# Two more heads in the Strassen products of one projection of a hybrid decoder layer

## The chip, the cores and the metric

The kernel runs on one core of a Trainium2 chip. The metric is the device time of one execution in microseconds (us). The kernel before takes 928.13 us, the median of three runs (927.85 to 928.35).

## What is computed

One layer of a trunk on 1024 tokens with 1024 channels: a state-space branch (S5) and a gated recurrent branch (RG-LRU, ten heads of 128 channels) are computed from one normalised input, projected, gated and added. The change concerns the projection of the second branch, `z_l`. From the reference, cut:

```python
s5_x, s5_g, lru_x, lru_g, gate_s, gate_l = jnp.split(proj, IN_SPLITS, axis=-1)
...
glu_a, glu_b = jnp.split(jax.nn.gelu(y_s) @ w_glu[i], 2, axis=-1)
y_s = glu_a * jax.nn.sigmoid(glu_b) * jax.nn.silu(s5_g)
z_s = y_s @ w_bs[i]
...
y_l = rg_lru(c, lru_w_a[i], lru_b_a[i], lru_w_x[i], lru_b_x[i], lru_lambda[i])
z_l = (y_l * jax.nn.silu(lru_g)) @ w_bl[i]
merged = jax.nn.sigmoid(gate_s) * z_s + jax.nn.sigmoid(gate_l) * z_l
x = x + rms_norm(merged @ w_out[i], g_post[i])
x = x + (p[i] @ w_ple[i]) * jax.nn.sigmoid(x @ w_ple_gate[i])
```

All data is float32, and `w_bl` has 1280 rows (ten heads) and 1024 columns.

## The kernel before, in words

Tensors lie with channels on the 128 partitions and the 1024 tokens along the free axis; a tile of 512 tokens is half a row (`HALF`). Matmuls run on rounded float32. To keep the precision, every operand is kept as a high part and a low part, the low one being the operand less its high part, and a product of two blocks is three matmuls of 128 x 128 by 128 x 512: high by high (L317), then high by low and low by high (L319), all in `three`. For activations `split` (L312, L313) makes the parts: ACT copies the high one, DVE subtracts for the low one.

**Weights.** A planner writes all weight blocks of 128 x 128 into one list and cuts it into quads of up to four blocks, in the order in which the products use them (`QUADS`). The class `Weights` brings each quad through four steps. `fetch` loads raw blocks on the SP queue into one of four raw buffers (a chunk of two blocks has a small buffer of its own). `sum` makes sums of raw blocks on POOL where Strassen's scheme wants them (L194). `make` puts the high part into one of six ring slots on ACT (L222). `lows` makes the low part on DVE (L234); for three weights behind the loop the low part comes from an accumulating DMA of POOL instead (L226). `next` hands out the quad that is due, `ahead` lets the steps run on by up to five quads. The instructions of all engines are in the order in which this code is written; only semaphores hold an engine back.

**The product with w_bl.** Heads 0 to 7 are seen as a matrix of two by two blocks: heads 0 to 3 and heads 4 to 7 in one direction, the two token halves in the other. Strassen's scheme in Winograd's form needs seven products for a pair of output rows. Each is over four blocks: 12 matmuls. Two of them, with operands B11 and B21, make a first stage (`bX`) that goes into the bank of psum `xs[p_]` for the four pairs p_; their sum is one output tile, and the first of them is kept in `bu`. The gated linear unit of the other branch comes in between (the GLU stage, `ysf`, `et`). Then a loop of four passes p_ does the other five products, with operands T2, T1, T3, B22 and T4, into banks z (`bZ`), w (`bW`) and v (`bV`). Behind T2, z gets `bu` added on DVE (L1322), and ACT copies it into u (L1323), which T3 needs as a start. Heads 8 and 9 are outside: `btail` adds their products, two blocks with six matmuls each time, to each output tile. Before the loop (`late_ops`) and while it runs, the operands T3, B22 and T4 are split, one tick at a time.

In one pass, PE does T2 (12 matmuls), T1 (12), the tail into v (6), T3 (12), the tail into w (6), B22 (12), the tail into z (6), T4 (12). DVE finishes output rows with `brow` (L1184), a product with the gates `ga` and `gb` that are read from DRAM.

```python
bprod(z, "T2", True)
V.tensor_tensor(z, z, u, ALU.add)
S.activation(u, z, AF.Copy)
bprod(w_, "T1", True)
S.activation(gb[:, HT:], w_, AF.Copy)
V.tensor_tensor(w_, w_, u, ALU.add)
tick()
...
btail(v, wb[2:], 1, True)
bmul(z, "T3", 2)
```

Gates for the stage of B11 and B21 are loaded from `sgl_d` on SP inside that stage, into tiles g0 and g1 of the pool `h2`. That pool's memory follows what was freed by the pool `l1` of the recurrent part.

Of the kernel before, what the change touches and what calls it, by code (L numbers as in the profile page):

```python
# [9 lines left out]
F32 = mybir.dt.float32  # L10
# [26 lines left out]
def weight_plan():  # L37
# [41 lines left out]
    for ks in (lo, hi2, hi):  # L79
        if ks is hi2:  # L80
            plain([b for m in range(0, ND, 2) for b in col("w_bl", m, hi2)])
            continue
        for m in (0, 4):
            plain(col("w_bl", m, ks) + col("w_bl", m + 2, ks))
    for j in range(NS):
        plain(col("w_glu", 4 + j, range(NS)) + col("w_glu", j, range(NS)))
    for m in range(0, ND, 2):
        c0, c1 = (chunk(col("w_bl", m + i, range(8))) for i in range(2))
        for part in ("O2", "S1", "P", "S3", "S4", "A22"):
            if part == "P":  # L90
                plain(col("w_bl", m, hi2) + col("w_bl", m + 1, hi2))
            else:
                quads.append((part, c0, c1, 4))
# [26 lines left out]
FIRST = ("O2",)  # L120


def chunk_users():
    last, begun = {}, {}
    for i, q in enumerate(QUADS):
        for c in q[1:2] if q[0] == "plain" else q[1:3]:
            if q[0] in FIRST or q[0] == "plain" and q[2] == 0:
                begun[c] = i
            last[begun[c], c] = i
    return last  # L130


LAST = chunk_users()


class Weights:
# [20 lines left out]
    def load(self, c):  # L157
        if c[1] == 2:
            t = self.tmp.tile([P, 2 * P], F32, tag="rawg", name=f"wraw{self.loads}")
        else:  # L160
            t = self.rawp.tile([P, 8 * P], F32, tag="raw", name=f"wraw{self.loads}")
        self.loads += 1
        self.nc.sync.dma_start(t[:, :c[1] * P], self.src[:, c[0] * P:(c[0] + c[1]) * P])
        return t

    def fetch(self, upto):
        while self.fetched <= min(upto, len(QUADS) - 1):
            q = QUADS[self.fetched]
            need = 2 if q[0] in FIRST else 1 if q[0] == "plain" and q[2] == 0 else 0
            small = need == 1 and q[1][1] == 2  # L170
            live = self.live[small] = [i for i in self.live[small] if i >= len(self.done) - len(self.owed)]
            if need + len(live) > (1 if small else self.RAW):
                return
            for c in q[1:1 + need]:
                live.append(LAST[self.fetched, c])
                self.raws[c] = self.load(c)
            self.fetched += 1

    def sum(self, upto):
        G = self.nc.gpsimd  # L180
        while len(self.ready) <= min(upto, len(QUADS) - 1):
# [14 lines left out]
            if q[0] == "plain":  # L196
                _, c, o, n = q
                self.ready.append((self.raws[c][:, o * P:(o + n) * P], n))
                continue
# [53 lines left out]
def tile_hybrid_trunk(  # L253
# [20 lines left out]
    page_pool = {i: pages for i in range(14)}  # L274
# [771 lines left out]
    yl, yl_raw = {}, {}  # L1046
    yr = []

    def yrow(k):
        if k % 2 == 0:  # L1050
            yr.append(page(6 + k // 2, f"yr{k // 2}", F32).rearrange("p (k n) -> p k n", k=2))
        return yr[k // 2][:, k % 2]
# [8 lines left out]
    def bq(q, k):  # L1061
        return yr[(k + 4 * (q // 20)) // 2][:, k % 2, HALF[q % 10 - 1]]

    def bsplit(name, k, src):
        hi, lo = bops[name]
        split(hi[:, k, :], lo[:, k, :], src)

    def lru_head(m):
# [33 lines left out]
        def late():  # L1102
# [11 lines left out]
            t = yrow(m) if m < 8 else l1.tile([P, NT], F32, tag=f"yr{m}", name=f"yr{m}")  # L1114
            V.tensor_tensor(t, sq, g, ALU.mult)  # L1115
            yl_raw[m] = t
# [32 lines left out]
    for m in (8, 9):  # L1149
        yl[m] = page(m - 4, f"yl{m}").rearrange("p (s n) -> p s n", s=2)  # L1150
        split(yl[m][:, 0], yl[m][:, 1], yl_raw[m])
# [21 lines left out]
    def bprod(ps, name, start):  # L1173
        W.ahead()
# [4 lines left out]
    def btail(ps, wb, h, start):  # L1179
        for k, w_ in zip((8, 9), wb):  # L1180
            three(ps, w_, (yl[k][:, 0, HALF[h]], yl[k][:, 1, HALF[h]]), start and k == 8, k == 9, not start)
# [17 lines left out]
    for p_ in range(4):  # L1199
        bprod(xs[p_], "B11", True)  # L1200
        S.activation(bu[:, p_, :], xs[p_], AF.Copy)
# [5 lines left out]
    for q in range(2):  # L1207
        W.ahead()
        wb = W.next()
        for i in range(2):  # L1210
            btail(xs[2 * q + i], wb[2 * i:2 * i + 2], 0, False)
# [9 lines left out]

    def t_ops():
        for k in range(4):
# [4 lines left out]
            V.tensor_tensor(bq(21, k), bq(21, k), t, ALU.subtract)  # L1228
            yield
        for k in range(4):  # L1230
# [46 lines left out]
    def late_ops():  # L1277
        for name, i, j, q in (("T3", 12, 13, 12), ("B22", 14, 15, 22), ("T4", 0, 1, 21)):
            bop(name, i, j)
            for k in range(4):  # L1280
                bsplit(name, k, bq(q, k))
# [28 lines left out]
    for p_ in range(4):  # L1310
# [9 lines left out]
        z, w_, v = (bank(f"b{n}{p_}") for n in "ZWV")  # L1320
        bprod(z, "T2", True)
        V.tensor_tensor(z, z, u, ALU.add)  # L1322
        S.activation(u, z, AF.Copy)  # L1323
        bprod(w_, "T1", True)
# [3 lines left out]
        W.ahead()  # L1328
        wb = W.next()
        btail(v, wb[2:], 1, True)  # L1330
        bmul(z, "T3", 2)
        S.activation(u, z, AF.Copy)
        V.tensor_tensor(v, v, gb[:, HT:], ALU.add)
        V.tensor_tensor(v, v, u, ALU.add)
        brow(m + 1, 1, ga[:, HALF[1]], v)
        tick()
        btail(w_, wb[:2], 1, False)
        bmul(w_, "B22", 2)
        brow(m, 1, gb[:, :HT], w_)
        tick()  # L1340
        btail(z, wb[2:], 0, False)
        bmul(z, "T4")
        brow(m + 1, 0, ga[:, HALF[0]], z)
# [354 lines left out]
```

## Time and profile before

| | |
|---|---|
| runs, median (low to high) | 928.13 us (927.85 to 928.35) |
| profiled execution | 928.25 us |
| its span | 926.5 us |
| PE busy | 919.0 us, 99% |
| DVE busy | 624.6 us, 67% |
| ACT busy | 469.1 us, 51% |
| POOL busy | 150.6 us, 16% |
| granted TensorE clock | 0.999 |

How to read it: the span is from the first to the last instruction of the profiled execution, and that execution took 1.75 us more than its span. Busy time is what the instructions of an engine cover. PE is TensorE's matmuls, DVE is VectorE, ACT is ScalarE, POOL is GpSimd, SP issues most of the DMAs. Numbers of lines, such as L313, are those of the kernel before.

### The profile page before, as it was taken

The page shows a single profiled execution, that of the slowest core. Times are in us where ns is not written, and L with a number is a line of the kernel's source. Part 1 is how long each engine was busy: PE and PEld are TensorE (multiplying, and loading weights), DVE is VectorE, ACT ScalarE, POOL GpSimd, SP SyncE. Part 2 cuts the span into 40 slices and gives each one's busy share as a digit, 9 for nine tenths or more (in the row PEclk, how much of TensorE's full clock was granted, in tenths as well). Part 3 has the DMA queues.
Part 4 walks back from the last instruction along what each step waited for, and adds up shares of the span by engine and source line. Part 5 has one row for each costly group of instructions (what it writes and reads, how often), then busy time and mean ns, then how long its engine had stood idle before and what let it go on. Part 6 is the DMA issues. An engine that isn't in the chain of part 4 may idle for free.

```text
span 926.5 us, 11716 instructions
## 1 busy us (share of the span) xinstructions
PE 919.0 (99%) x4228; PEld 760.3 (82%) x4228; DVE 624.6 (67%) x977; ACT 469.1 (51%) x714; POOL 150.6 (16%) x159
## 2 busy tenths in 40 slices
PE   9999999999999999999999999999999999999997
PEld 7888888888888888888888888888888887887886
DVE  6885566666664347766666767687862798886863
ACT  6643233444443356666666668544534355558531
POOL 1218112212220000000000000022322126422100
PEclk9999999999999999999999999999999999999999
DMA  9745445564533201111111116811479975499951
GB/s 358 277 126 160 126 142 166 172 171 133 173 97 113 74 29 52 52 46 51 52 52 52 47 34 216 291 56 55 141 255 244 247 193 206 119 245 233 301 184 56
DMA packets 70442, 134.21 MB, mean 145 GB/s; under 512 B 18416, under 2 KB 32880, under 8 KB 70384
## 3 DMA queue, kind: packets, MB, share of 16 engines
q1 hardware_dynamic: 64768, 122.72, 41.7%
q0 software_dynamic: 5472, 10.49, 6.3%
q8 instruction: 33, 0.54, 0.2%
q10 hardware_dynamic: 144, 0.26, 0.1%
q14 instruction: 25, 0.20, 0.1%
HBM read 95.30 MB, written 27.53 MB: 133 GB/s over the span
## 4 chain that ended last, share of the span: by engine, by line
PE 89%; issue 6%; DMA 2%; DVE 1%; POOL 1%; ACT 0%; POOLq 0%; SPq 0%
PE ps_L L319 16%; PE ps_L L317 8%; PE ps_rx L319 8%; PE ps_rg L319 8%; PE ps_rg L317 4%; PE ps_rx L317 4%; PE ps_F L319 3%; PE ps_u L319 3%; PE bZ L319 3%; PE ps_pg L319 2%; PE bW L319 2%; PE pg L319 2%; PE bX L319 2%; PE ps_ple L319 2%; PE ps_ea L319 2%
## 5 line engine op out<-in xcount | busy, mean ns | idle before, releaser
L319 PE MATMUL ps_L<-hB,wq 128*128 128x512 f32 x640 | 197.4, 390 | 0.0
L319 PEld LDWEIGHTS ps_L<-hB,wq 128*128 128x128 f32 x640 | 120.3, 188 | 24.3
L317 PE MATMUL ps_L<-hB,wq 128*128 128x512 f32 x320 | 127.1, 397 | 0.0
L222 ACT ACTIVATE wq<-wraw 128x512 fp32r<-128x512 f32 (+1 forms) x188 | 112.5, 613 | 24.1 <-issue 9.2
L234 DVE TENSOR_TENSOR wq<-wraw,wq 128x512 fp32r<-128x512 f32 (+1 forms) x152 | 105.0, 706 | 3.1 <-ACT wq L222 3.1
L319 PE MATMUL ps_rg<-hB,wq 128*128 128x512 f32 x320 | 98.5, 389 | 0.0
L319 PE MATMUL ps_rx<-hB,wq 128*128 128x512 f32 x320 | 98.5, 389 | 0.0
L319 PE MATMUL ps_pg<-x1hl,wq 128*128 128x512 f32 x240 | 74.9, 392 | 0.3 <-DVE x1hl L1374 0.2
L317 PEld LDWEIGHTS ps_L<-hB,wq 128*128 128x128 f32 x320 | 60.2, 188 | 13.3 <-issue 1.7
L319 PEld LDWEIGHTS ps_rg<-hB,wq 128*128 128x128 f32 x320 | 60.1, 188 | 12.5
L319 PEld LDWEIGHTS ps_rx<-hB,wq 128*128 128x128 f32 x320 | 60.1, 188 | 12.4
L194 POOL TENSOR_TENSOR wS<-wraw 128x512 f32<-128x512 f32 x8 | 12.4, 1549 | 354.8 <-DMA wraw<-w_blocks 343.3
L1078 DVE SCALAR_TENSOR_TENSOR c<-ps_rx,cp_t,c 128x1023 f32<-128x1023 f32 (+2 forms) x30 | 38.5, 1282 | 46.2 <-ACT c L1076 45.5
L317 PE MATMUL ps_rx<-hB,wq 128*128 128x512 f32 x160 | 62.3, 389 | 0.0
L317 PE MATMUL ps_rg<-hB,wq 128*128 128x512 f32 x160 | 62.3, 389 | 0.0
L319 PEld LDWEIGHTS ps_pg<-x1hl,wq 128*128 128x128 f32 x240 | 44.8, 188 | 11.5 <-DVE x1hl L1374 1.7
L1015 ACT ACTIVATE sg<-ps_L 128x1024 f32<-128x1024 f32 x20 | 20.5, 1027 | 59.7 <-issue 52.5
L226 POOL DMA_DIRECT2D wq<-wraw x36 | 31.8, 883 | 100.1 <-ACT wq L225 65.6
L317 PE MATMUL ps_pg<-x1hl,wq 128*128 128x512 f32 x120 | 47.0, 391 | 0.0
L319 PE MATMUL ps_u<-hB,wq 128*128 128x512 f32 x128 | 39.8, 392 | 0.4 <-DVE hB L736 0.4
L319 PE MATMUL ps_F<-ys,wq 128*128 128x512 f32 x128 | 39.4, 389 | 0.0
L1086 ACT ACT_TABLE_LOAD x9 | 11.5, 1283 | 51.2 <-DVE yr L1115 51.2
(360 smaller groups left out, 1927.0 us busy)
## 6 DMA issues: line engine op xcount, KB each, us to landing
wraw<-w_blocks SPq DMA_DIRECT2D x95, 512.0 KB
wq<-wraw POOLq DMA_DIRECT2D x36, 256.0 KB, 6.0
xt<-x_t SPq DMA_DIRECT2D x8, 512.0 KB
ple_d<-ple_sb SPq DMA_DIRECT2D x8, 512.0 KB
wn<-sbt SPq DMA_DIRECT2D x8, 512.0 KB
sgl_d<-sg SPq DMA_DIRECT2D x8, 512.0 KB
wn<-pt_d SPq DMA_DIRECT2D x16, 256.0 KB
sgs_d<-sg SPq DMA_DIRECT2D x8, 512.0 KB
```

Source lines behind the costliest of these rows:

```text
L194: G.tensor_tensor(s[name], s[a], s[b], op)
L222: nc.scalar.activation(hi, src, AF.Copy)
L226: nc.gpsimd.dma_start(lo.bitcast(F32), src, accum_op=ALU.add)
L234: self.nc.vector.tensor_tensor(lo, src, hi.bitcast(F32), ALU.subtract)
L317: T.matmul(ps, wh, xh, start=start, stop=False, skip_group_check=more)
L319: T.matmul(ps, a, b, start=False, stop=stop and a is (wh if xl_last else wl), skip_group_check=more)
L1015: S.activation(t, ps, AF.Sigmoid)
L1078: V.scalar_tensor_tensor(c[:, d:], ps[:, :NT - d], w_[3 - d], c[:, d:], ALU.mult, ALU.add)
L1086: S.activation(sq, ps, AF.Sigmoid)
```

## The change

Heads 8 and 9 become a fifth block of each of Strassen's seven products instead of plain tails: head 8 beside heads 0 to 3, head 9 beside heads 4 to 7. Each product is over five blocks, 15 matmuls, the last three by `bextra`. The tails in the loop and bank v go. The other operand of each product, the sum of heads, gets a fifth block in `bx` (page 19 holds heads 8 and 9, `yx`; the extra block of T4 stays in a psum bank, `t4x`). For the weights there are two new kinds of quads per pass: XS, four blocks of the extra block's sums, made by four operations on 128 x 128 on DVE one behind the other, and X22, the block alone. They come from two new small raw buffers of five blocks. The scratch of dynamic DMAs is 4096 bytes instead of its default of 16384, which moves all pools in SBUF down. The pool h2 no longer lies on l1's memory, and the four loads of gates in the stage of B11 and B21 move on the SP queue from that stage to right behind the stores of `y_d`. Cut to the core:

```diff
     hi2 = range(8, NL)
     for ks in (lo, hi2, hi):
         if ks is hi2:
-            plain([b for m in range(0, ND, 2) for b in col("w_bl", m, hi2)])
+            plain([("w_bl", k, m) for k in hi2 for m in range(0, ND, 2)])
...
     for m in range(0, ND, 2):
         c0, c1 = (chunk(col("w_bl", m + i, range(8))) for i in range(2))
-        for part in ("O2", "S1", "P", "S3", "S4", "A22"):
-            if part == "P":
-                plain(col("w_bl", m, hi2) + col("w_bl", m + 1, hi2))
-            else:
-                quads.append((part, c0, c1, 4))
+        cx = chunk([("w_bl", k, d) for k, d in ((9, m), (8, m), (8, m + 1), (9, m + 1))])
+        quads.extend((("O2", c0, c1, 4), ("XS", cx, 0, 4)))
+        quads.extend((part, c0, c1, 4) for part in ("S1", "S3", "S4", "A22"))
+        quads.append(("X22", cx, 3, 1))
...
+SINGLE = ("plain", "XS", "X22")
+
+
+def begins(q):
+    return 2 if q[0] in FIRST else int(q[0] in SINGLE and q[2] == 0)
...
 def chunk_users():
     last, begun = {}, {}
     for i, q in enumerate(QUADS):
-        for c in q[1:2] if q[0] == "plain" else q[1:3]:
-            if q[0] in FIRST or q[0] == "plain" and q[2] == 0:
+        for c in q[1:2] if q[0] in SINGLE else q[1:3]:
+            if begins(q):
                 begun[c] = i
             last[begun[c], c] = i
     return last
 LAST = chunk_users()
+SMALL = {q[1] for q in QUADS if q[0] == "XS" or q[1][1] == 2}
...
     def load(self, c):
-        if c[1] == 2:
-            t = self.tmp.tile([P, 2 * P], F32, tag="rawg", name=f"wraw{self.loads}")
+        if c in SMALL:
+            t = self.tmp.tile([P, 5 * P], F32, tag="rawg", name=f"wraw{self.loads}", bufs=2)
         else:
             t = self.rawp.tile([P, 8 * P], F32, tag="raw", name=f"wraw{self.loads}")
         self.loads += 1
+        if c[1] == 4 and c in SMALL:
+            for o, n in ((0, 3), (3, 1)):
+                self.nc.sync.dma_start(t[:, (o + o // 3) * P:(o + o // 3 + n) * P],
+                                       self.src[:, (c[0] + o) * P:(c[0] + o + n) * P])
+            return t
         self.nc.sync.dma_start(t[:, :c[1] * P], self.src[:, c[0] * P:(c[0] + c[1]) * P])
         return t
     def fetch(self, upto):
         while self.fetched <= min(upto, len(QUADS) - 1):
             q = QUADS[self.fetched]
-            need = 2 if q[0] in FIRST else 1 if q[0] == "plain" and q[2] == 0 else 0
-            small = need == 1 and q[1][1] == 2
+            need = begins(q)
+            small = need == 1 and q[1] in SMALL
             live = self.live[small] = [i for i in self.live[small] if i >= len(self.done) - len(self.owed)]
-            if need + len(live) > (1 if small else self.RAW):
+            if need + len(live) > (2 if small else self.RAW):
                 return
             for c in q[1:1 + need]:
...
+            if q[0] in SINGLE:
+                r = self.raws[q[1]]
+                if q[0] == "X22":
+                    self.ready.append((r[:, 4 * P:], 1))
+                    continue
+                a12, a11, a21, s1, a22 = (r[:, j * P:(j + 1) * P] for j in range(5))
+                for d, a, b, op_ in ((s1, a21, a22, ALU.add), (a21, a11, a21, ALU.subtract),
+                                     (a11, s1, a11, ALU.subtract), (a12, a12, a11, ALU.subtract)):
+                    self.nc.vector.tensor_tensor(d, a, b, op_)
+                self.ready.append((r[:, :HT], 4))
                 continue
...
-        if k % 2 == 0:
+        if k == 8:
+            yr.append(page(19, "yx", F32).rearrange("p (k n) -> p k n", k=2))
+        elif k % 2 == 0:
...
     def bq(q, k):
+        if k == 4:
+            return yr[4][:, q // 20, HALF[q % 10 - 1]]
         return yr[(k + 4 * (q // 20)) // 2][:, k % 2, HALF[q % 10 - 1]]
+    bx = {}
+
     def bsplit(name, k, src):
-        hi, lo = bops[name]
-        split(hi[:, k, :], lo[:, k, :], src)
+        split(*bx[name], src) if k == 4 else split(*(t[:, k, :] for t in bops[name]), src)
+
+    def bx_at(name, t, i):
+        bx[name] = t[:, i, :], t[:, i + 1, :]
...
-    for m in (8, 9):
-        yl[m] = page(m - 4, f"yl{m}").rearrange("p (s n) -> p s n", s=2)
-        split(yl[m][:, 0], yl[m][:, 1], yl_raw[m])
+    bx4, bx5 = (quarter(page(i, f"bx{i}")) for i in (4, 5))
+    bx_at("B11", bx4, 0)
+    bx_at("B21", bx4, 2)
+    bsplit("B11", 4, bq(11, 4))
+    bsplit("B21", 4, bq(21, 4))
+    V.tensor_tensor(bq(11, 4), bq(12, 4), bq(11, 4), ALU.subtract)
+    V.tensor_tensor(bq(12, 4), bq(22, 4), bq(12, 4), ALU.subtract)
...
-    def bprod(ps, name, start):
-        W.ahead()
+    def bprod(ps, name, start, held=1):
+        W.ahead(held)
         hi, lo = bops[name]
         for k, wb in enumerate(W.next()):
             three(ps, wb, (hi[:, k, :], lo[:, k, :]), start and k == 0, k == 3, not start)
-    def btail(ps, wb, h, start):
-        for k, w_ in zip((8, 9), wb):
-            three(ps, w_, (yl[k][:, 0, HALF[h]], yl[k][:, 1, HALF[h]]), start and k == 8, k == 9, not start)
+    def bextra(ps, wb, name):
+        three(ps, wb, bx[name], False, True, True)
...
         bprod(xs[p_], "B11", True)
-        S.activation(bu[:, p_, :], xs[p_], AF.Copy)
...
-    for q in range(2):
+    for name in ("B11", "B21"):
         W.ahead()
-        wb = W.next()
-        for i in range(2):
-            btail(xs[2 * q + i], wb[2 * i:2 * i + 2], 0, False)
+        for p_, wb in enumerate(W.next()):
+            bextra(xs[p_], wb, name)
+            if name == "B11":
+                S.activation(bu[:, p_, :], xs[p_], AF.Copy)
         tick()
...
+    t4x = []
+
     def t_ops():
-        for k in range(4):
+        bx_at("T2", bx5, 0)
+        for k in range(5):
             t = btmp[:, k % 2, :]
             V.tensor_tensor(t, bq(22, k), bq(11, k), ALU.subtract)
             bsplit("T2", k, t)
             yield
-            V.tensor_tensor(bq(21, k), bq(21, k), t, ALU.subtract)
-            yield
-        for k in range(4):
+            if k == 4:
+                t4x.append(px.tile([P, HT], F32, tag="px", name="t4x"))
+            V.tensor_tensor(t4x[0] if k == 4 else bq(21, k), bq(21, k), t, ALU.subtract)
+            yield
+        bx_at("T1", bx5, 2)
+        for k in range(5):
             bsplit("T1", k, bq(11, k))
...
     def late_ops():
         for name, i, j, q in (("T3", 12, 13, 12), ("B22", 14, 15, 22), ("T4", 0, 1, 21)):
             bop(name, i, j)
-            for k in range(4):
-                bsplit(name, k, bq(q, k))
+            if name == "T4":
+                bx_at(name, quarter(page(19, "bx19")), 0)
+            else:
+                bx_at(name, bx4, 0 if name == "T3" else 2)
+            for k in range(5):
+                bsplit(name, k, t4x[0] if name == "T4" and k == 4 else bq(q, k))
...
-        z, w_, v = (bank(f"b{n}{p_}") for n in "ZWV")
+        z, w_ = (bank(f"b{n}{p_}") for n in "ZW")
         bprod(z, "T2", True)
+        W.ahead()
+        wx = W.next()
+        bextra(z, wx[1], "T2")
         V.tensor_tensor(z, z, u, ALU.add)
         S.activation(u, z, AF.Copy)
-        bprod(w_, "T1", True)
+        bprod(w_, "T1", True, 2)
+        bextra(w_, wx[3], "T1")
         S.activation(gb[:, HT:], w_, AF.Copy)
         V.tensor_tensor(w_, w_, u, ALU.add)
         tick()
-        W.ahead()
-        wb = W.next()
-        btail(v, wb[2:], 1, True)
         bmul(z, "T3", 2)
-        S.activation(u, z, AF.Copy)
-        V.tensor_tensor(v, v, gb[:, HT:], ALU.add)
-        V.tensor_tensor(v, v, u, ALU.add)
-        brow(m + 1, 1, ga[:, HALF[1]], v)
+        bextra(z, wx[2], "T3")
+        V.tensor_tensor(gb[:, HT:], gb[:, HT:], z, ALU.add)
+        brow(m + 1, 1, ga[:, HALF[1]], gb[:, HT:])
         tick()
-        btail(w_, wb[:2], 1, False)
         bmul(w_, "B22", 2)
+        bextra(w_, wx[0], "B22")
         brow(m, 1, gb[:, :HT], w_)
         tick()
-        btail(z, wb[2:], 0, False)
         bmul(z, "T4")
+        W.ahead()
+        bextra(z, W.next()[0], "T4")
         brow(m + 1, 0, ga[:, HALF[0]], z)
...
-    nc = bacc.Bacc("TRN2", target_bir_lowering=False, num_devices=1)
+    nc = bacc.Bacc("TRN2", target_bir_lowering=False, num_devices=1, dynamic_dma_scratch_size=4096)
```

The instructions that the prediction speaks of stand on DVE. The first place is from the last product of the GLU stage (`ysf`) to the addition of `bu` into w (`bW`). In it `bT` is the low part of T3's operand, `bx` that of an extra block, `wq` the low part of a quad. Before:

```order
L1272 TENSOR_TENSOR ysf_4668<-et,ps_ea_4932 128x4x128
L1272 TENSOR_TENSOR ysf_4668<-et,ps_ea_4933 128x4x128
L313 TENSOR_TENSOR bT_4968<-yr_2940,bT_4967 128x512 x2
L313 TENSOR_TENSOR bT_4968<-yr_3277,bT_4967 128x512 x2
L234 TENSOR_TENSOR wq_4934<-wraw_4682,wq_4934 128x512
L1322 TENSOR_TENSOR bZ_4981<-bZ_4981,bu 128x512
L234 TENSOR_TENSOR wq_4984<-wS_120_4796,wq_4984 128x512
L234 TENSOR_TENSOR wq_5001<-wraw_4682,wq_5001 128x512
L1326 TENSOR_TENSOR bW_4982<-bW_4982,bu 128x512
```

and now:

```order
L1307 TENSOR_TENSOR ysf_4669<-et,ps_ea_4950 128x4x128
L1307 TENSOR_TENSOR ysf_4669<-et,ps_ea_4951 128x4x128
L334 TENSOR_TENSOR bT_4984<-yr_2942,bT_4983 128x512 x2
L334 TENSOR_TENSOR bT_4984<-yr_3279,bT_4983 128x512 x2
L334 TENSOR_TENSOR bx_4442<-yx,bx_4442 128x512
L255 TENSOR_TENSOR wq_4952<-wraw_4683,wq_4952 128x512
L255 TENSOR_TENSOR wq_5001<-wS_120_4798,wq_5001 128x512
L1364 TENSOR_TENSOR bZ_4999<-bZ_4999,bu 128x512
L1369 TENSOR_TENSOR bW_5000<-bW_5000,bu 128x512
```

A split of the extra block of T3 stands ahead, and the two quads' low parts stand ahead of the addition into z (`bZ`, L1364) instead of one; the raw quad's low part that stood third is later now.

The second place is behind it, up to the splits of T4: `bB` is B22's operand, `bT` is T4's, `ga` and `gb` the gates, `wraw` the raw weights. Before:

```order
L313 TENSOR_TENSOR bB_5024<-yr_3614,bB_5023 128x512 x2
L313 TENSOR_TENSOR bB_5024<-yr_3947,bB_5023 128x512 x2
L1333 TENSOR_TENSOR bV_4983<-bV_4983,gb_4978 128x512
L1334 TENSOR_TENSOR bV_4983<-bV_4983,bu 128x512
L1184 TENSOR_TENSOR ga_4977<-ga_4977,bV_4983 128x512
L313 TENSOR_TENSOR bT_5061<-yr_3614,bT_5060 128x512 x2
L313 TENSOR_TENSOR bT_5061<-yr_3947,bT_5060 128x512 x2
```

and now:

```order
L334 TENSOR_TENSOR bB_5042<-yr_3616,bB_5041 128x512 x2
L334 TENSOR_TENSOR bB_5042<-yr_3949,bB_5041 128x512 x2
L334 TENSOR_TENSOR bx_4442<-yx,bx_4442 128x512
L255 TENSOR_TENSOR wq_5016<-wraw_4683,wq_5016 128x512
L255 TENSOR_TENSOR wq_5053<-wraw_4685,wq_5053 128x128
L218 TENSOR_TENSOR wraw_4842<-wraw_4842 128x128 x4
L1373 TENSOR_TENSOR gb_4996<-gb_4996,bZ_4999 128x512
L1213 TENSOR_TENSOR ga_4995<-ga_4995,gb_4996 128x512
L334 TENSOR_TENSOR bT_5088<-yr_3616,bT_5087 128x512 x2
L334 TENSOR_TENSOR bT_5088<-yr_3949,bT_5087 128x512 x2
L334 TENSOR_TENSOR bx_5089<-t4x,bx_5089 128x512
```

Ahead of the splits of T4 there are now the low parts of two quads, the four chained operations on 128 x 128 (L218), and the addition of z into gb (L1373), on which the product with ga depends; the two additions into bank v are gone.

## Rows read from the trace of the kernel before

**Rows 1.** The page, first part: engine, busy us (share of the span), instructions.
```profile
span 926.5 us, 11716 instructions
PE 919.0 (99%) x4228; PEld 760.3 (82%) x4228; DVE 624.6 (67%) x977; ACT 469.1 (51%) x714; POOL 150.6 (16%) x159
```
**Rows 2.** PE's waits, first and last of five: line, releaser, us, times, longest us.
```profile
PE warm L500 <- DVE halfpi L291: 1.1, 1, 1.1
...
PE ps_pg L319 <- DVE x1hl L1374: 0.2, 1, 0.2
```
**Rows 3.** PE's timeline: start us, us, line and operation; loop's first matmul, first behind it.
```profile
637.83 0.39 PE L317 MATMUL bZ<-bT,wq 128*128 128x512 f32 x1
...
708.55 0.39 PE L317 MATMUL ps_F<-ys,wq 128*128 128x512 f32 x1
```
**Rows 4.** Windows: GLU stage, first, third, fourth pass: us; PE, PEld, DVE, ACT, POOL busy (count); clock.
```profile
600.00:637.00 37.00, 37.00 (x165) 30.67 (x164) 26.28 (x30) 17.43 (x27) 7.52 (x5) 1.00 0.22 74
637.80:655.50 17.70, 17.70 (x79) 14.64 (x78) 16.97 (x25) 9.07 (x17) 3.97 (x3) 1.00 0.16 50
...
673.20:690.90 17.70, 17.70 (x80) 14.66 (x79) 12.95 (x17) 6.70 (x12) 5.98 (x4) 1.00 0.68 224
690.90:708.50 17.60, 17.60 (x79) 14.60 (x78) 6.56 (x10) 7.74 (x14) 4.46 (x5) 1.00 0.93 265
```
**Rows 5.** DVE's timeline in the first pass: start us, us, instruction, [idle before, releaser].
```profile
639.47 2.47 DVE L313 TENSOR_TENSOR bT<-yr,bT 128x512 fp32r<-128x512 f32 x4
...
642.48 0.68 DVE L1322 TENSOR_TENSOR bZ<-bZ,bu 128x512 f32<-128x512 f32 x1
...
644.34 1.38 DVE L234 TENSOR_TENSOR wq<-wraw,wq 128x512 fp32r<-128x512 f32 x1 [0.59 <-ACT wq L222]
645.64 0.69 DVE L1326 TENSOR_TENSOR bW<-bW,bu 128x512 f32<-128x512 f32 x1
646.25 2.99 DVE L313 TENSOR_TENSOR bB<-yr,bB 128x512 fp32r<-128x512 f32 x4
649.16 0.69 DVE L1333 TENSOR_TENSOR bV<-bV,gb 128x512 f32<-128x512 f32 x1
649.95 0.70 DVE L1334 TENSOR_TENSOR bV<-bV,bu 128x512 f32<-128x512 f32 x1
650.69 0.69 DVE L1184 TENSOR_TENSOR ga<-ga,bV 128x512 f32<-128x512 f32 x1
```
**Rows 6.** ACT's timeline in the first pass: the copy of z.
```profile
643.19 0.60 ACT L1323 ACTIVATE bu<-bZ 128x512 f32<-128x512 f32 x1 [6.10 <-DVE bZ L1322]
```
**Rows 7.** POOL's timeline in the first pass: the second and third sum.
```profile
643.88 1.29 POOL L194 TENSOR_TENSOR wS<-wS,wraw 128x512 f32<-128x512 f32 x1 [12.15 <-issue]
645.14 1.74 POOL L194 TENSOR_TENSOR wraw<-wraw,wraw 128x512 f32<-128x512 f32 x1
```
**Rows 8.** Small operations on DVE: groups by shape (busy, mean ns), and one line's instructions.
```profile
L1615 DVE TENSOR_TENSOR sbp<-sbp,x 128x128 f32<-128x128 f32 x2 | 0.6, 292 | 0.1
...
L402 DVE TENSOR_SCALAR sdp<-ident,rs_pre x8: 279/283/287, 27.9 to 29.2; 128x128 f32<-128x128 f32 x8
```
**Rows 9.** DVE's timeline in the second pass: two low parts.
```profile
654.90 1.47 DVE L234 TENSOR_TENSOR wq<-wS,wq 128x512 fp32r<-128x512 f32 x1
...
660.57 1.11 DVE L234 TENSOR_TENSOR wq<-wraw,wq 128x512 fp32r<-128x512 f32 x1 [0.59 <-ACT wq L222]
```
**Rows 10.** SP's timeline: the stores of y_d and the next issue.
```profile
297.25 2.57 SPq L988 DMA_DIRECT2D y_d<-ysb  x4
304.39 0.33 SPq L1019 DMA_DIRECT2D sil_d<-sg  x1
```
**Rows 11.** The page: POOL's queue (packets, MB, share), issue cost by line, issue to landing.
```profile
q0 software_dynamic: 5472, 10.49, 6.3%
...
L226 POOL DMA_DIRECT2D wq<-wraw x36 | 31.8, 883 | 100.1 <-ACT wq L225 65.6
...
wq<-wraw POOLq DMA_DIRECT2D x36, 256.0 KB, 6.0
```
**Rows 12.** POOL's timeline in the second pass: the first sum.
```profile
659.73 1.40 POOL L194 TENSOR_TENSOR wS<-wraw 128x512 f32<-128x512 f32 x1 [3.91 <-DMA wraw<-w_blocks]
```

More of the change, by code (lines that the diff above doesn't have):

```diff
@@ L198, in sum @@
                 self.ready.append((self.raws[c][:, o * P:(o + n) * P], n))
+                continue
[3 more added lines that the diff above has]
+                    self.ready.append((r[:, 4 * P:], 1))
+                    continue
+                a12, a11, a21, s1, a22 = (r[:, j * P:(j + 1) * P] for j in range(5))
[3 more added lines that the diff above has]
+                self.ready.append((r[:, :HT], 4))
                 continue
@@ L273, in tile_hybrid_trunk @@
     pages = ctx.enter_context(tc.tile_pool(name="pages", bufs=1))
-    page_pool = {i: pages for i in range(14)}
+    page_pool = {i: pages for i in (*range(14), 19)}
     def page(i, name, dt=F32R):
@@ L1045, in tile_hybrid_trunk @@
     l1 = lctx.enter_context(tc.tile_pool(name="l1", bufs=1))
-    yl, yl_raw = {}, {}
     yr = []
     def yrow(k):
-        if k % 2 == 0:
+        if k == 8:
+            yr.append(page(19, "yx", F32).rearrange("p (k n) -> p k n", k=2))
+        elif k % 2 == 0:
             yr.append(page(6 + k // 2, f"yr{k // 2}", F32).rearrange("p (k n) -> p k n", k=2))
@@ L1113, in late @@
             yield
-            t = yrow(m) if m < 8 else l1.tile([P, NT], F32, tag=f"yr{m}", name=f"yr{m}")
-            V.tensor_tensor(t, sq, g, ALU.mult)
-            yl_raw[m] = t
+            V.tensor_tensor(yrow(m), sq, g, ALU.mult)
             yield
```

## The prediction

> **What bounds the kernel now.** I read the page first. TensorE (PE) is busy 919.0 of the 926.5 us span [rows 1], so the question is only how many matmuls are issued and how often the next one is late. The list of PE's waits answers the second half: five waits in the whole span, the longest 1.1 us, 2.8 us together (the first and the last are shown) and none of them in the w_bl loop [rows 2]. There PE runs without a gap: the first matmul of the loop starts at 637.83, the first of the stage behind it at 708.55, and between them lie 4 x 78 = 312 matmuls [rows 3], so one costs (708.55 - 637.83) / 312 = 0.2267 us. This is the price of a matmul below; the 0.39 us of a row is a modelled, overlapping length.
>
> The windows by pass then show who could stop PE. In the first pass of the loop DVE is busy 16.97 of 17.70 us; in the third it is 12.95 and in the fourth 6.56 [rows 4]. So the first pass has hardly any room on DVE, and the later ones have 4.7 us or more. The rest rests on DVE's own timeline in that first pass.
>
> A measurement of this kernel can tell about 0.2% from no change, 1.86 us; I use that as the bound of "same".
>
> **Part 1: the matmuls.** In the stage of B11 and B21 the count is the same: four tails of two blocks become eight blocks, 24 matmuls either way. In the loop a pass had five products of four blocks (T2, T1, T3, B22, T4: 60 matmuls) and three tails of two blocks (18), together 78. Now it has five products of five blocks: 75. Three fewer in each of four passes: 12 x 0.2267 = **-2.72 us**. PE is full there, so all of it is on the path.
>
> **Part 2: the third product of the first pass (T3).** T3 stands behind 30 matmuls before and after (12 + 12 + 6; now 15 + 15), so it is due at 637.83 + 30 x 0.2267 = 644.63 [rows 3], as before. Its first matmul adds into z and has to wait for ACT's copy of z to u. Before, DVE left the GLU product at 639.47, made T3's four splits in 2.41 us (0.60 each), one low part, and started z's add at 642.48 [rows 5]; ACT began the copy at 643.19, 0.71 us after that start, and took 0.60 [rows 6]. It was ready at 643.79, so 0.84 us early. Now a fifth split and the low part of S4's quad stand ahead of z's add (first pair of pieces in the section on the change): 639.47 + 5 x 0.60 + 2 x 0.60 = 643.68, and the copy is ready at 643.68 + 0.71 + 0.60 = 644.99. With the 0.04 us that the semaphore takes T3 starts at 645.03: **+0.4 us**, between 0.3 and 0.5.
>
> **Part 3: the last product of the first pass (T4).** It stands 30 matmuls behind T3: due at 645.03 + 6.80 = 651.83. Its first matmul now waits for the new addition of z into gb (DVE reads z, PE overwrites it), its second for the low part of T4's first split. DVE's queue up to there, second pair of pieces:
> - w's add waits for ACT's copy of w to gb, which can't start before T1's last matmul has ended and the copy of z is over (644.93); 0.60 us on, it starts at 645.53 (before 645.64 [rows 5]).
> - B22's splits from 646.13. Before, four took 2.91 us (646.25 to 649.16) where 2.41 would do; the 0.50 us is the third POOL sum, which ran until 646.88 [rows 7]. For five I take 3.01 plus 0.26 (half, since the sum may start earlier or later): 649.4.
> - the low part of A22's quad 0.60, that of the single block X22 0.19, which is the distance at which independent operations of that size start (eight from 27.9 to 29.2 [rows 8]): 650.2.
> - the four operations on 128x128 that make the extra block's sums, each waiting for the one before. A tensor_tensor of that size lasts 0.292 us [rows 8]; a dependent successor starts 0.04 to 0.10 us after the end (649.95 + 0.70 to 650.69, 649.16 + 0.69 to 649.95 [rows 5]). At 0.33 each 1.3 us: 651.5.
> - the addition of z into gb, 0.69 us: 652.2. T4's first matmul starts 0.4 us late.
> - ga's product depends on that addition and starts at 651.5 + 0.79 = 652.3, T4's first split at 652.9, ready at 653.55. T4's second matmul, due at 652.06, starts at 653.6. From there DVE gives a split every 0.60 us and PE uses one every 0.68, so nothing more is lost.
>
> Together **+1.5 us**. If the POOL sum no longer meets the splits and the four small operations follow each other without a gap (0.19 each) it is 0.7; if the sum costs 0.75 and each small operation 0.39, 2.2. I take 1.5, since the gaps between dependent operations are measured.
>
> A rule bears on the stretch. The row says that the low part which started at 644.34 lasted 1.38 us instead of 0.67 [rows 5], while POOL ran its sum from 643.88 to 645.17 [rows 7]; operations with a PSUM operand, such as w's add (0.69), were not stretched. The Trainium skill (SBUF — State Buffer, section "SBUF: two separate sides") states that VectorE and GpSimd share a port pair as an exclusive lock, held for the whole instruction, and that a VectorE operation with two SBUF inputs has to wait for a GpSimd operation that reads SBUF. The trace agrees: 643.88 + 1.29 to the end of 644.34 + 1.38 leaves 0.55, one undisturbed operation. By that rule, part 4 would be 0.4 us instead of 0, and the sum 0.4 us later.
>
> **Part 4: the passes behind it.** The backlog of the first pass enters the second: T4's splits end at 655.8, then two products, three low parts, the product with z, a split of ys and two low parts stand ahead of z's add, which comes at about 661.5 and lets T3 go at about 662.8 to 664.0 (POOL sums took 0.8 and 0.4 us from two such low parts [rows 9]). T3 of the second pass is due at 653.6 + 44 x 0.2267 = 663.5. So 0, at most 0.5. The third and fourth pass have 4.7 and 11 us of idle DVE [rows 4]: 0.
>
> **What costs nothing, and what hides it.** Behind the loop nothing is changed but the queue position of the next weights; no PE wait stood there. In the GLU stage DVE gets four more 512-column operations (2.4 us) and ACT two: DVE was idle 37.00 - 26.28 = 10.7 us there [rows 4]. Without that cover they would delay T2's first matmul by up to 2.4. ACT loses a copy of z in each pass and gets three splits in the first. On SP the extra block's load is two transfers instead of one, and four loads of gates move from the B11 stage to right behind the y stores; SP issued nothing there from 299.8 to 304.4 [rows 10].
>
> **Sum.** -2.72 + 0.4 + 1.5 + 0 = -0.8 us. The profiled execution took 928.25 us, 0.12 above the median of the runs (928.13). It becomes 927.4, on the median **927.3 us**. With the bounds (0.3 to 0.5, 0.7 to 2.2, 0 to 0.5) the forecast's own range is 926.4 to 928.6.
>
> **Rivals.**
> A: no stall. If DVE's work reaches T3 and T4 in time, because it leaves the GLU stage earlier than at 639.47 (its last operations there may come sooner) and POOL's sums fall elsewhere, the whole 2.72 us stays: 925.4 on the median. For it: PE waited nowhere in the loop, and my chain adds up seven estimates. Against it: DVE had 0.73 us of room in the first pass [rows 4], and three splits (1.8), a new addition in place of two (-0.7), and the four sums (1.3) are added to it. Chance 0.22.
>
> B: the quarter of scratch limits POOL's transfers. 36 low parts for the stages behind the loop are made by POOL's accumulating DMAs, 256 KB and 6.0 us each from issue to landing, 0.88 us to issue [rows 11]. A quad of w_bs feeds 24 matmuls, 5.44 us of PE. If only one such transfer could be in flight, a quad would come every 6.9 us, 1.45 us late: 8 quads of w_bs cost 11.6 us (939), all 36 cost 52 (979). From two in flight it costs nothing. No row tells how much of the scratch a transfer takes; the only one near it is the count of packets, 5472 / 36 = 152 a transfer over 16 engines [rows 11], about 10 each. Chance 0.05. The Trainium skill (DMA: Bandwidth & Descriptors, "Terms") has descriptors of 16 bytes, written to rings in SBUF; by it 4,096 bytes would hold 256 of them, an estimate, and B would not come about; no run here shows it.
>
> C: slower, by one wait that repeats. The four sums of the extra block are in DVE's queue, where POOL's stood in its own. If their raw block lands late, everything behind them on DVE waits: gb's addition, T4's splits, and so PE. In the second pass POOL's first sum waited 3.91 us for raw weights [rows 12], so loads there can be just in time. A stall like part 3's largest in each pass, 4 x 1.9 = 7.6, gives 928.25 - 2.72 + 7.6 = 933.1. It decides from 0.68 us a pass (slower than before at all) and 1.15 (by more than the bound). Against it: the extra blocks have two buffers of their own, and so are asked for more than a pass ahead. Chance 0.07.
>
> **Chances.** Forecast 0.62, A 0.22, B 0.05, C 0.07, and 0.04 for what I do not see, counted as no change. The range takes in the forecast and A: 925.2 to 928.7. Faster by over 0.2% (below 926.27): A and 0.03 of the forecast, 0.25. Slower by over 0.2% (above 929.99): B and C, 0.12. Same: 0.63.
>
> **What would show it.** Right, if PE's waits in the new profile have two rows in the first pass of the loop, one on ACT's copy of z of about 0.4 us and one or two on DVE at T4 of about 1.5 together, if the loop is about 70.7 - 0.8 us long, and if DVE is busy nearly without a gap from 637 to 656. Wrong, if the loop has no PE wait (A), if PE waits at the first w_bs matmuls on POOL's transfers (B), or if there is a wait at T4 in every pass with DVE idle ahead of the 128x128 operations (C).

## The result, and the profile after

The changed kernel takes 930.18 us in the median of 22 runs (928.21 to 932.9); the kernel before, run beside it, takes 928.3 (927.85 to 929.4, also 22). The ratio is 1.0022 with a 95% interval of 1.0014 to 1.0030: slower by 1.9 us, at the edge of what I had called no change, and outside the range of the forecast. The runs of the changed kernel also lie 4.7 us apart, those of the kernel before 1.6.

The first part of the page after the change, which answers to [rows 1]:

```profile
span 928.0 us, 11731 instructions
PE 917.5 (99%) x4216; PEld 757.2 (82%) x4216; DVE 631.6 (68%) x1002; ACT 470.2 (51%) x719; POOL 150.1 (16%) x159
```

Twelve matmuls fewer, as counted, and 1.5 us less of PE. This execution took 929.8 us, 1.55 more than the one profiled before. PE's waits (line, releaser; us in total, times, longest), where [rows 2] had five:

```profile
PE oX L340 <- DMA wq<-wraw: 1.7, 1, 1.7
PE warm L521 <- DVE halfpi L312: 1.1, 1, 1.1
PE bZ L340 <- DVE bT L334: 0.8, 1, 0.8
...
PE bZ L338 <- ACT bu L1365: 0.3, 1, 0.3
```

The two waits on `bZ` are those that the prediction named. The largest, on `oX`, is in the stage of w_out, 60 us behind the loop, and no step of mine led there. PE's timeline puts places to them (start us, us, instruction, idle before and releaser):

```profile
637.51 0.39 PE L338 MATMUL bZ<-bT,wq 128*128 128x512 f32 x1
...
644.76 0.50 PE L338 MATMUL bZ<-bT,wq 128*128 128x512 f32 x1 [0.29 <-ACT bu L1365]
...
653.06 0.73 PE L340 MATMUL bZ<-bT,wq 128*128 128x512 f32 x2 [0.76 <-DVE bT L334]
...
707.68 0.39 PE L338 MATMUL ps_F<-ys,wq 128*128 128x512 f32 x1
...
767.51 0.50 PE L340 MATMUL oX<-mB,wq 128*128 128x512 f32 x1 [1.70 <-DMA wq<-wraw]
...
769.92 0.39 PE L338 MATMUL oY<-mT,wq 128*128 128x512 f32 x1
```

The first `oY` of the kernel before:

```profile
768.39 0.39 PE L317 MATMUL oY<-mT,wq 128*128 128x512 f32 x1
```

Against the kernel before, the loop starts 0.32 us earlier (637.51 for 637.83; over the profiles of all ten kernels this start lies between 637.51 and 638.25), and takes 70.17 us instead of 70.72, so 0.55 less. From the first `ps_F` to the first `oY` it is 62.24 us, where it was 768.39 - 708.55 = 59.84: 2.40 more. Behind that nothing changes (158.1 us to the end in both). -0.32 - 0.55 + 2.40 = +1.53, which is the difference of the spans (1.5). So the loop did gain, and more than four times its gain was lost behind it.

The place of the loss is in the chain of waits, between 712 and 728 us (start us, us, what):

```profile
712.64 1.16 DVE mg L1461 x2
713.79 5.66 DMA ms_d<-ga
...
719.52 7.10 DMA msr<-ms_d
...
726.71 0.70 DVE mg L1463
```

`ms_d` holds the gated rows of the w_bl branch in DRAM. The last of them is stored from ga (tile g0), and a row that is read back (`msr`) takes the same tile. The rows are numbered in the order of their use; 0 and 1 are fetched in another way, rows with an even number take g0, where ga was, and odd ones g1, where gb was. Row 2, the first one needed, must wait until ga's last store has landed. SP's queue, first after the change and then before it:

```profile
707.30 0.42 SPq L1214 DMA_DIRECT2D ms_d<-gb  x1
712.88 0.32 SPq L1444 DMA_DIRECT2D msr<-ms_d  x1
713.37 0.33 SPq L173 DMA_DIRECT2D wraw<-w_blocks  x1
713.79 0.39 SPq L1214 DMA_DIRECT2D ms_d<-ga  x1
719.52 0.32 SPq L1444 DMA_DIRECT2D msr<-ms_d  x1
```

```profile
708.82 0.41 SPq L1185 DMA_DIRECT2D ms_d<-gb  x1
710.86 0.33 SPq L163 DMA_DIRECT2D wraw<-w_blocks  x1
711.28 0.45 SPq L1185 DMA_DIRECT2D ms_d<-ga  x1
714.08 2.15 SPq L1404 DMA_DIRECT2D msr<-ms_d  x2
```

Before, both stores go out and then both loads. After, the load of row 3 stands ahead of the last store. It waits 5.6 us for gb's store to land, everything on SP waits with it, and ga's store, whose data DVE had ready at 708.57 (L1213: 707.88 + 0.69), leaves at 713.79. Row 2 is asked for at 719.52, where both rows had been by 716.23. DVE's timeline shows the cost, and that the rest follows from it:

```profile
723.52 0.69 DVE L1461 TENSOR_TENSOR mg<-gsp,ps_F 128x512 f32<-128x512 f32 x1 [4.07 <-PE ps_F L340]
726.71 0.69 DVE L1463 TENSOR_TENSOR mg<-mg,msr 128x512 f32<-128x512 f32 x1 [2.50 <-DMA msr<-ms_d]
```

In the kernel before, DVE came to the same row 1.60 us sooner and did not wait:

```profile
725.11 0.69 DVE L1423 TENSOR_TENSOR mg<-mg,msr 128x512 f32<-128x512 f32 x1
```

From there to 762 us DVE is busy nearly without a gap in both. ACT splits what DVE has made and then makes the high part of the next quad whose low part comes from POOL, and POOL's transfer waits for that high part. The last of these transfers for w_out, before and after:

```profile
761.87 0.86 POOL L226 DMA_DIRECT2D wq<-wraw  x1 [3.00 <-ACT wq L225]
```

```profile
763.61 0.87 POOL L247 DMA_DIRECT2D wq<-wraw  x1 [3.15 <-ACT wq L246]
```

It leaves 1.74 us later, and PE meets it at 767.51. No line of the diff touches the loads and stores on SP that began this: their order in the queue came out differently when the program was built. In the code the last store of ga stands ahead of both loads, so the sentence of the section on the kernel before, that the instructions of all engines are in the order of the code, does not hold for SP.

### The profile page after: what moved, and what is told of

Read it like the earlier page. It is cut to its first block, busy times and chain, and to the rows that moved or that the text cites. A ratio compares the mean times of both kernels' runs of the same rounds, so it can differ in the third digit from the quotient of the medians.

```text
span 928.0 us, 11731 instructions
## 1 busy us (share of the span) xinstructions
PE 917.5 (99%) x4216; PEld 757.2 (82%) x4216; DVE 631.6 (68%) x1002; ACT 470.2 (51%) x719; POOL 150.1 (16%) x159
## 4 chain that ended last, share of the span: by engine, by line
PE 83%; issue 7%; DVE 4%; DMA 3%; POOL 2%; ACT 1%; POOLq 0%; ACTq 0%; DVEq 0%; SPq 0%
PE ps_L L340 16%; PE ps_L L338 8%; PE ps_rg L340 8%; PE ps_rx L340 8%; PE ps_rg L338 4%; PE ps_rx L338 4%; PE ps_pg L340 3%; PE ps_u L340 3%; PE bZ L340 3%; PE bX L340 2%; PE pg L340 2%; PE bW L340 2%; PE ps_ple L340 2%; PE ps_eb L340 2%; PE ps_ea L340 2%
## 5 line engine op out<-in xcount | busy, mean ns | idle before, releaser
L255 DVE TENSOR_TENSOR wq<-wraw,wq 128x512 fp32r<-128x512 f32 (+2 forms) x156 | 103.0, 677 | 1.7 <-ACT wq L243 1.7
```

The lines of the kernel that those rows point to most:

```text
L255: self.nc.vector.tensor_tensor(lo, src, hi.bitcast(F32), ALU.subtract)
```

## The experiments

Theory **M**: the order on SP costs the time. Rivals: **S**, the smaller scratch slows POOL's transfers (B of the prediction), and **L**, the new load on DVE in the loop is all of it. The first four runs tell them apart.

**e1_swap.** The two rows change tiles, nothing else; only SP's order moves.

```diff
-            msr[n] = h2.tile([P, NT], F32, tag=f"g{n % 2}", name=f"msr{n}")
+            msr[n] = h2.tile([P, NT], F32, tag=f"g{1 - n % 2}", name=f"msr{n}")
```

> The changed kernel, but the gate rows that are read back behind the loop (msr) take the other of the two tiles g0 and g1, so that on SP the load of row 2 (needed first) follows the store of gb and the load of row 3 follows the last store of ga; the other four engines' programs are the same. Theory M (the order of four transfers on SP behind the loop costs the time): DVE's wait for msr at the third gate row goes, PE's wait of 1.7 us in the w_out stage (oX) goes with it, the stage from the first ps_F to the first oY falls from 62.2 us to 59.8, and the time is 927.4 (927.0 to 927.9), 0.9 below the kernel before, with runs within about 1.5 us of each other. Theory S (the smaller scratch slows POOL's transfers): no change, 930.2 and runs 4 us apart. Theory L (the loop's load on DVE is the cause): no change, 930.2.

Measured: 928.04 us (927.37 to 929.04), ratio to before 0.9996 (0.9987 to 1.0005). From 930.18 that is 2.1 us, and the runs are 1.7 us apart: M, against S and L. But 0.6 us of what M promised is missing. `ps_F` to `oY` did fall to 59.95 us, and the wait for row 2 is gone; row 4 is now late, on DVE:

```profile
737.77 0.69 DVE L1463 TENSOR_TENSOR mg<-mg,msr 128x512 f32<-128x512 f32 x1 [0.76 <-DMA msr<-ms_d]
```

Row 4 takes row 2's tile, so it is loaded only when row 2 has been used (726.48 on SP), and 11 us were too short. PE then waits 1.1 us at `oY`.

**e2_scratch.** `dynamic_dma_scratch_size=4096` in the kernel before, and no other edit.

> The kernel before with a quarter of the dynamic DMA scratch and nothing else; the order of every engine is the same. Theory M and theory L: 928.3 (within 0.4), no PE wait on a transfer of low parts. Theory S: 930 or more, PE waits on POOL's transfers, and the runs lie 3 us or more apart.

Measured: 928.51 us (927.95 to 929.65), ratio 1.0002 (0.9993 to 1.0011). S falls for the kernel before; e5_page, below, has the small scratch too and loses nothing behind the loop. No wait of PE on a transfer appears in its profile. That profile is of the slowest of its runs (929.65), and in it DVE does wait for a later row:

```profile
738.69 0.69 DVE L1423 TENSOR_TENSOR mg<-mg,msr 128x512 f32<-128x512 f32 x1 [0.59 <-DMA msr<-ms_d]
```

PE then waits 1.1 us at `oY`. So the kernel before has little to spare at these rows either, with its own order on SP.

**e3_order.** The order of the changed kernel, put into the kernel before (shortened: `ms_load` is also moved up and made to load a row once):

```diff
         bmul(z, "T4")
+        if p_ == 3:
+            ms_load(3)
         brow(m + 1, 0, ga[:, HALF[0]], z)
```

> The kernel before, with the load of gate row 3 (msr) written ahead of the last store of ga, so that on SP it stands in front of that store as it does in the changed kernel; the other engines' programs are the same. Theory M: the store of ga waits some 5 us for the store of gb to land, row 2 is loaded after that, DVE waits about 2.5 us for it, PE waits in the w_out stage, and the time is 930.5 (929.5 to 932) with runs 3 us or more apart. Theories S and L: 928.3, as before.

Measured: 928.65 us (927.92 to 933.21), ratio 1.0008 (0.9998 to 1.0019): not clear of no change, and my 930.5 was too much. Three of its eleven runs (929.64, 931.03 and 933.21) lie above every run of before in that comparison (up to 929.58), and in the profiled one DVE did not wait:

```profile
713.25 0.32 SPq L1315 DMA_DIRECT2D msr<-ms_d  x1
713.66 0.38 SPq L1185 DMA_DIRECT2D ms_d<-ga  x1
718.28 0.32 SPq L1315 DMA_DIRECT2D msr<-ms_d  x1
```

The store landed in 4.6 us here, in 5.7 in the changed kernel. Row 2 was asked for 1.2 us earlier than there (718.28 for 719.52), and PE came to these rows 1.3 us later (first `ps_F` at 708.94 for 707.68): together the 2.5 us that DVE waited in the changed kernel. Of the 1.3 us only 0.55 are the loop's gain; the rest is that the loop began at 638.22 here. So in the profiled run the order alone cost nothing, and the three long runs have no profile. That the changed kernel has less to spare, and therefore pays in most of its runs, is argued from these profiles, not shown by a run of its own.

**e4_swap_pool.** e1_swap with the extra block's four sums on POOL.

```diff
-                    self.nc.vector.tensor_tensor(d, a, b, op_)
+                    G.tensor_tensor(d, a, b, op_)
```

> The first run's kernel, with the four sums on 128x128 of each extra block on POOL instead of DVE. If the wait at the last product (T4) of the first pass comes from DVE's queue as the prediction has it, four such operations (1.3 us) less ahead of T4's first split take most of that wait of 1.3 us: 926.3 (925.9 to 926.8), about 1.1 us below the first run. If POOL's sums then meet DVE's splits and stretch them by as much, or the sums come too late there, 927.4 or more.

Measured: 928.32 us (927.91 to 929.46), ratio to before 1.0003 (0.9994 to 1.0011): a miss. PE's waits at T4 of the first pass were not smaller, but one more was there:

```profile
652.35 0.47 PE L338 MATMUL bZ<-bT,wq 128*128 128x512 f32 x1 [0.26 <-DVE gb L1373]
653.59 0.73 PE L340 MATMUL bZ<-bT,wq 128*128 128x512 f32 x2 [0.77 <-DVE bT L334]
```

The second matmul of T4 is 1.56 us late here (due 31 matmuls behind T3's first, 645.00), 1.27 in e1_swap: what DVE was spared, 1.26 us, came back, as the expectation's second half had it. B22's four splits, beside POOL's sums, took 4.13 us; in e1_swap they took 2.66:

```profile
646.08 4.13 DVE L334 TENSOR_TENSOR bB<-yr,bB 128x512 fp32r<-128x512 f32 x4
```

```profile
646.28 2.66 DVE L334 TENSOR_TENSOR bB<-yr,bB 128x512 fp32r<-128x512 f32 x4
```

The loop took 70.27 us, against 69.97 in e1_swap. The run's time says less than the loop's, since the profile, of its slowest run, shows the loss behind the loop again, with e1_swap's order. The store of ga took 8.7 us to land, row 4 came late, and PE waited 1.5 us at `oX`:

```profile
715.29 0.38 SPq L1214 DMA_DIRECT2D ms_d<-ga  x1
724.04 0.32 SPq L1444 DMA_DIRECT2D msr<-ms_d  x1
...
739.02 0.69 DVE L1463 TENSOR_TENSOR mg<-mg,msr 128x512 f32<-128x512 f32 x1 [1.87 <-DMA msr<-ms_d]
```

So the better order alone does not cure every run.

**e5_page.** Theory M2, two more tiles. Page 19 is free behind T4 (shortened):

```diff
-            msr[n] = h2.tile([P, NT], F32, tag=f"g{n % 2}", name=f"msr{n}")
+            if n == 2:
+                msrx.append(page(19, "msrx", F32).rearrange("p (k n) -> p k n", k=2))
+            msr[n] = msrx[0][:, n % 2] if n < 4 else h2.tile([P, NT], F32, tag=f"g{n % 2}", name=f"msr{n}")
```

> The changed kernel, with the gate rows 2 and 3 that are read back behind the loop (msr) in page 19, which is free after T4's last matmul, and rows 4 and 5 in g0 and g1, where rows 2 and 3 were; no load of row 2 or 3 waits for a store of ga or gb, and rows 4 and 5 are loaded when those stores have landed, not when rows 2 and 3 have been used. Theory M2 (what is lost behind the loop is the order and the two tiles: each row's load waits for the row or the store ahead of it): DVE waits for no msr, PE has no wait in the w_out stage above 0.4 us, the time is 927.5 (927.1 to 927.9), 0.9 below the kernel before, which is what the loop itself is shorter. Theory BW (the transfers behind the loop are limited by their sum, so time gained ahead of them is given back wherever the loads stand): waits for msr or gsp stay, 928.0 or more.

Measured: 927.27 us (927.10 to 927.74), ratio to before 0.9989 (0.9980 to 0.9998). No wait for `msr` is left, and the runs are within 0.6 us. M2 holds, BW falls. SP's queue:

```profile
707.43 0.46 SPq L1214 DMA_DIRECT2D ms_d<-gb  x1
707.94 0.45 SPq L1446 DMA_DIRECT2D msrx<-ms_d  x1
...
712.59 0.88 SPq L1214 DMA_DIRECT2D ms_d<-ga  x1
713.52 0.48 SPq L1446 DMA_DIRECT2D msrx<-ms_d  x1
...
718.96 0.32 SPq L1446 DMA_DIRECT2D msr<-ms_d  x1
```

Row 2 is asked for at 707.94, 11.6 us sooner than in the changed kernel. The stores are no quicker: row 4 still has to wait for ga's, and is loaded 6.4 us behind it (718.96), but it is not needed so soon.

**e7_before_page.** The same page in the kernel before, in the room that the smaller scratch leaves.

> The kernel before with a quarter of the scratch, and in the room that this gives a page for gate rows 2 and 3 as in run e5_page: their loads wait for no store of ga or gb. It tells how much of e5_page's time is due to the page and how much to the change. If the order of SP behind the loop cost the kernel before nothing, 928.4 (within 0.3), and the change with the page is worth 1.1 us; if the kernel before also lost there in most of its runs, 927.6 to 928.0 with the runs closer together (within 0.8 us), and the change with the page is worth 0.3 to 0.7.

Measured: 928.33 us (928.05 to 929.09), ratio 1.0001 (0.9992 to 1.0009). The page is worth nothing that can be measured to the kernel before, so the 1.1 us of e5_page (0.2 to 1.9 by its interval) are the change's own.

**e6_page_early.** e5_page with the fifth splits of T3 and B22 in the GLU stage (shortened):

```diff
             bsplit("T1", k, bq(11, k))
+            if k < 2:
+                name, q = (("T3", 12), ("B22", 22))[k]
+                bx_at(name, bx4, 2 * k)
+                bsplit(name, 4, bq(q, 4))
             yield
...
-            for k in range(5):
+            for k in range(5 if name == "T4" else 4):
```

> The kernel of the run before, with the splits of the fifth block of T3 and B22 made in the GLU stage, where DVE is idle, instead of in the first pass of the loop: two splits (1.2 us) less on DVE ahead of T4, one (0.6) less ahead of T3. If the two waits of the first pass come from DVE's queue as the prediction has it, T3's wait (0.45 us late) goes and T4's (1.3 us) falls to 0.3 or less, so the loop is 1.5 us shorter; with M2 all of it stays: 926.0 (925.6 to 926.6). With BW: 927.5 to 928, and DVE's waits for msr grow by what the loop gains. If the loop's waits have another cause, the time is that of the run before.

Measured: 926.41 us (926.06 to 926.63), ratio to before 0.9979 (0.9970 to 0.9987): the best version, and faster than both kernels. T3's wait is gone, and T4's is down, but not to 0.3; its second matmul, due 31 matmuls behind T3's first at 651.60, still is 0.86 us late:

```profile
644.57 0.39 PE L338 MATMUL bZ<-bT,wq 128*128 128x512 f32 x1
...
652.46 0.74 PE L340 MATMUL bZ<-bT,wq 128*128 128x512 f32 x2 [0.66 <-DVE bT L334]
```

The expectation took both splits off T4's wait. But T3's split stands ahead of w's addition, which has to wait for ACT's copy of w in any case. In e5_page and here:

```profile
645.43 0.70 DVE L1369 TENSOR_TENSOR bW<-bW,bu 128x512 f32<-128x512 f32 x1 [1.15 <-ACT gb L1368]
```

```profile
645.39 0.70 DVE L1371 TENSOR_TENSOR bW<-bW,bu 128x512 f32<-128x512 f32 x1 [1.69 <-ACT gb L1370]
```

What was saved ahead of it became idle time of DVE, so only B22's split helped T4: its second matmul came 0.80 us earlier (652.46 for 653.26), and, T3 now being on time, was due 0.39 earlier.

**e8_all.** e6_page_early with the product behind T4's splits:

```diff
-        brow(m + 1, 1, ga[:, HALF[1]], gb[:, HT:])
         tick()
+        brow(m + 1, 1, ga[:, HALF[1]], gb[:, HT:])
```

> The kernel of e6_page_early with the product of gate and row (ga) written behind T4's splits instead of ahead of them: one operation of 0.60 us less ahead of T4's first split. T4's second matmul, still 0.84 us late in e6_page_early, should come 0.6 earlier: 925.8 (925.5 to 926.2). If something else holds it (ACT's high parts, the addition into gb), no change: 926.4.

Measured: 926.32 us (926.07 to 926.82), ratio to before 0.9979 (0.9970 to 0.9988): no change beside e6_page_early. T4's second matmul did come at 651.90, 0.56 earlier. It was given back within the next pass's first product, where a quad's low part, behind the product that was moved, is late:

```profile
651.90 0.74 PE L340 MATMUL bZ<-bT,wq 128*128 128x512 f32 x2
...
656.11 0.50 PE L340 MATMUL bZ<-bT,wq 128*128 128x512 f32 x1 [0.28 <-DVE wq L255]
```

## Why the prediction was wrong, point by point

- **Part 1 (-2.72) holds.** In the third and fourth pass no wait is left, and T2 starts at 673.68, 690.68 and `ps_F` at 707.68 in the profile after: 17.00 us each, 75 x 0.2267. Before it was 17.68. T2's first matmul in the second, third and fourth pass:

```profile
656.40 0.39 PE L338 MATMUL bZ<-bT,wq 128*128 128x512 f32 x1
...
673.68 0.39 PE L338 MATMUL bZ<-bT,wq 128*128 128x512 f32 x1
...
690.68 0.39 PE L338 MATMUL bZ<-bT,wq 128*128 128x512 f32 x1
```

- **Part 2 (+0.4) holds.** T3 was due at 637.51 + 6.80 = 644.31 and started at 644.76: 0.45. With this wait and the next, rival A is out.
- **Part 3 (+1.5) holds, 0.2 too high.** The first matmul of T4 was 0.27 late (651.83 against 644.76 + 6.80), the second 1.27 (653.06 against 651.79). The four small operations took 1.17 us to the start of gb's addition, for 1.3 that I had. Taking away two splits (e6_page_early) took away T3's wait and 0.4 us of T4's, so the cause is DVE's queue.
- **Part 4 (0, at most 0.5) holds.** The second pass took 17.28 us (656.40 to 673.68), 0.28 over. z's addition came at 661.96, for 661.5 that I had. Ahead of it a low part took 1.77 us beside a POOL sum that ran from 656.69 to 658.37, and a split 1.40 beside the next sum:

```profile
657.13 1.77 DVE L255 TENSOR_TENSOR wq<-wS,wq 128x512 fp32r<-128x512 f32 x1
...
659.43 1.40 DVE L334 TENSOR_TENSOR ys<-ysf,ys 128x512 fp32r<-128x512 f32 x1
```

  The Trainium skill (SBUF — State Buffer, "SBUF: two separate sides") has VectorE and GpSimd hold their shared port pair for a whole instruction. The row agrees: 1.77 us is the rest of the sum (1.24) and 0.53 of its own. By that rule I had worked out 0.4 for this part, which is nearer to the 0.28 than the 0 that I took.
- **The loop's sum** was -0.8, and -0.55 was measured (70.17 us for 70.72), -0.72 in e5_page (70.00). With the loss behind it removed, e5_page takes 927.27, where the forecast was 927.3. That the two agree so closely is in part luck: beside e5_page the kernel before took 928.38, so the gain is 1.1 us, of which its profile puts 0.72 in the loop; the rest lies ahead of it and behind it, where I had forecast nothing.
- **The step that failed** is the sentence "Behind the loop nothing is changed but the queue position of the next weights; no PE wait stood there." It cost 2.4 us. Two things are wrong in it. The order on SP behind the loop did change: one load moved ahead of one store, which the order of the built program showed and I did not read there, since I took every engine's instructions to stand in the order of the code and had followed SP only at the places that the diff names. And I looked at PE's waits alone. In the trace of before nothing waits for `msr`, but DVE is busy nearly without a gap for 37 us from its first use of `msr` (725.11) on, so a later row passes on to PE. Nor had the chances a place for it: the 0.04 for what I did not see was counted as no change.
- **Rival B** named the kind of wait that was to come, PE on one of POOL's transfers, but in the stage of w_bs, where it came in that of w_out, and with the wrong cause: such a transfer was late because its high part was, not for want of scratch (e2_scratch, e5_page). Its estimate of 256 places for descriptors did not settle it as I wrote: two transfers have 304 packets [rows 11], and no row tells how many places a packet takes. The two runs settle it. **Rival C** is excluded by the third and fourth pass. Its 1.9 us is parts 2 and 3 together; part 3's largest was 2.2.

## What to carry to other kernels

Compare the order of every queue in the built program, also at stages that the diff does not touch, and look in each for a load that waits for a store to land and stands ahead of a store that is ready. Where such a load and store share a tile, tiles of their own for the rows needed first were worth more here than a better order (927.27 us in e5_page against 928.04 in e1_swap): they removed the wait and the scatter of the runs. And where no wait stands in the trace there can still be no slack: ask what starts the next stretch in which an engine is busy throughout.

## What was not expected of the hardware

A store of 256 KB to DRAM held the load that waited for it by 4.6 us in e3_order, 5.7 in the changed kernel, 6.4 in e5_page and 8.7 in e4_swap_pool, by SP's issue times, in the same place. Runs of the changed kernel, with two such pairs one behind the other ahead of a full engine, were 4.7 us apart; with later rows behind these stores, which are not needed so soon, they were within 0.6 us (e5_page). A quarter of the dynamic DMA scratch cost nothing that could be measured for 36 accumulating transfers of 256 KB (e2_scratch, ratio 1.0002, 0.9993 to 1.0011).
